# One core: k projected ahead of q, two sum banks from pair 4 on, small turns on sum banks, and GpSimd's multiplications on VectorE

## The chip, the core and the metric

The kernel runs on one core of one Trainium2 chip. The metric is device time in microseconds; the median of several runs is compared. The core has five engines with a queue each: TensorE (PE, with its weight loads as PEld), VectorE (DVE), ScalarE (ACT), GpSimd (POOL) and SyncE (SP, which here only starts transfers). Each queue runs in the order in which it was written; engines wait for one another by semaphores.

## What is computed

One layer of a trunk with two token mixers, on x of 1024 x 1024, all in float32:

```
h = rmsnorm(x, norm_g) * (1 + scale) + shift            # shift, scale, gate from c @ w_ada + b_ada
q_a, k_a, v_a, z_a, q_b, k_b, v_b, z_b, f_logit, g_logit = split(h @ w_in)
y_a = stick_breaking(q_a, k_a, v_a)                     # 8 heads of 64, strictly causal
y_a = (y_a * silu(z_a)) @ w_o_sb
cum_log_f = cumsum(log_sigmoid(f_logit + b_forget))
y_b = softmax(q_b k_b / 8 + cum_log_f[t] - cum_log_f[s]) v_b   # 8 heads of 64, causal
y_b = (y_b * silu(z_b)) @ w_o_fox
g = sigmoid(g_logit + b_gate)
merged = g[0] * y_a + g[1] * y_b
out = rmsnorm(x + gate * (merged @ w_out), final_g)
```

## The kernel before

Channels lie on the 128 partitions, and the 16 heads are worked through as 8 pairs: pairs 0 to 3 are the stick-breaking heads, 4 to 7 the forgetting ones. Every float32 product is made of three matmuls of split operands (a high part and a remainder). A projection unit fills one PSUM bank of 128x512 (an "acc" tile) with 24 matmuls, lines L181 to L183; the loads of its weights go through `load_w`.

For each pair p there are two runs of `attention(p, j)`, one for each head j. A run goes from the longest blocks of rows (m = 3) to the shortest (m = 0). A block computes its scores into z tiles (L623, L625; four banks in a ring, shared with the "tp" tiles for transposes), works them into weights on ACT and DVE (L690 to L726), sends the weights through a transposing transfer (wT) and, some steps later, multiplies them with v (`pv`, L756 and L757, into one bank "pv"). `turn` transposes the result (L776), gates it (L778) and stores it. Between the pieces of a run, a filler writes projection units into PE's queue: z, v, the merge gates and the next pair's q and k. So what stands between two blocks is the work of the next pair and of the gates. The steps at which `pv` and `turn` come are the numbers PVAT, PVFIRST, TURNAT and TURNEND; `sprinkle` puts small jobs (`load_v`, `largest`, `spread`, `take_v`) at counted steps of those units. The framework's scheduler then sets the final order on each engine, so that written order and run order can differ.

`largest` finds a power of two above the largest v of two pairs (transpose at L467, chain of small DVE operations up to vpow, L475); `spread` copies it to all partitions by a matmul (L480) and a copy (L482). `forget_gates` transposes the logits of the forget gate (L571). `residual_gate` sums a product of w_ada over eight loads (L599, gacc) and turns it with a matmul (L606). All four take a tp tile, one of the four of the z ring. `evac_q` and `evac_k` split a projected bank into two heads: on ACT the copies (L380, L383), on DVE the remainders (L381 for k, L384 for q); `evac_k` then starts the transfers kx<-ks (L404, L405) from GpSimd's queue. `evac_z` and `evac_g` do a chain on ACT and DVE (L409 to L413, then L423 for z); the last reader of a z bank is L423, that of a gate's bank of j < 8 is L412, and a gate of j >= 8 is only copied (L431).

The sum banks are a ring, and the v products have one bank that alternates only once "late" is set:

```
ring = {"next": 0, "of": 2, "pv": False, "late": False}
...
    ring["pv"] = ring["late"] and not ring["pv"]
    return acc_tile(2) if ring["pv"] else ps_pv.tile([P, 512], F32, name="pv", tag="pv")
...
    if b is None:
        b = ring["next"]
        ring["next"] = (b + 1) % ring["of"]
    return ps_acc.tile([P, 512], F32, name="acc", tag="acc%d" % b)
```

Until pair 7 the ring runs over three banks; then it has two, and the third takes every other v product. Pair 7's fill is the output projection of the first branch (`out_a`, L904 multiplies its sums with the gates in mA), then that of the second branch (`out_b`, L981 and L983), and at the end the product with w_out and the final norm.

Of the kernel before, what the change touches and what calls it, by code (L numbers as in the profile page):

```python
# [18 lines left out]
P = 128  # L19
S = 1024  # L20
D = 1024
HD = 64
# [27 lines left out]
T7 = (27, 27)  # L50
# [5 lines left out]
OUTQ = (0, 0)  # L56
LAGS = ((1, 2, 3, 4), (0, 1, 2, 3))
PVAT = (18, 16, 14, 10)
PVFIRST = 12
TURNAT = (22, 20, 18, 14)  # L60
TURNEND = (21, 19, 17, 13)

# [6 lines left out]
def tile_hybrid_block(ctx, tc, x, c, w_ada, b_ada, norm_g, w_in, b_forget,  # L69
# [380 lines left out]
        return (QA if p < 4 else QB) + (p % 4) * P  # L450

    def proj_qk(p):
        return proj(qcol(p), evac_q, p) + proj(qcol(p) + 512, evac_k, p)

    fT = [None]

# [6 lines left out]
    def largest(p):  # L463


        pt = tp_tile()
        nc.tensor.transpose(pt[0:1, :P], vmost[p], ident)  # L467
        top = at.tile([1, 1], F32, name="vtop", tag="vtop", bufs=2)
        nc.vector.tensor_reduce(top, pt[0:1, :P], mybir.AxisListType.X, ALU.max)
        nc.vector.tensor_scalar(top, top, 1e-25, None, ALU.max)  # L470
        e = top.bitcast(I32)
        nc.vector.tensor_scalar(e, e, 0x7F800000, None, ALU.bitwise_and)
        pair = vscale[p] = at.tile([1, 2], F32, name="vpow", tag="vpow", bufs=2)
        nc.vector.tensor_scalar(pair[:, 0:1].bitcast(I32), e, -1.0, float((254 + VSCALE) << 23), ALU.mult, ALU.add)
        nc.vector.tensor_scalar(pair[:, 1:2].bitcast(I32), e, 1.0, float((VSCALE + 15) << 23), ALU.mult, ALU.subtract)  # L475

    def spread(p):

        pt = tp_tile()
        nc.tensor.matmul(pt[:, 0:2], ones_row, vscale[p], start=True, stop=True)  # L480
        o = at.tile([P, 2], F32, name="vsc", tag="vsc", bufs=2)
        nc.vector.tensor_copy(o, pt[:, 0:2])  # L482
        for q in (p, p + 1):
            vscale[q], vback[q] = o[:, 0:1], o[:, 1:2]
# [82 lines left out]


    def forget_gates():
        pt = tp_tile()  # L570
        nc.tensor.transpose(pt[:64, :P], fT[0].rearrange("p h a -> p (h a)"), ident)  # L571
        fo = stage()[:64, 0:P]
        nc.vector.tensor_copy(fo, pt[:64, :P])
        nc.sync.dma_start(fd.rearrange("h (a t) -> (h a) t", a=TB), fo)
        fl = at.tile([8, S], F32, name="fl", tag="fb", bufs=2)
        nc.sync.dma_start(fl, fd)
        nc.vector.tensor_scalar(fl, fl, bfg, None, ALU.add)
        fa = at.tile([8, S], F32, name="fa", tag="fb", bufs=2)
        nc.scalar.activation(fa, fl, AF.Abs)
        nc.scalar.activation(fa, fa, AF.Exp, scale=-1.0)  # L580
        nc.scalar.activation(fa, fa, AF.Ln, bias=1.0)
        nc.vector.scalar_tensor_tensor(fa, fl, 0.0, fa, ALU.min, ALU.subtract)
        nc.vector.tensor_tensor_scan(fl, fa, fa, 0.0, ALU.add, ALU.bypass)
        nc.sync.dma_start(fd, fl)


    def residual_gate():

        box, raw = [], {}

        def load(k):
            raw[k] = load_raw(wada[k * P:(k + 1) * P, 2 * D:3 * D], [P, D])

        def weigh(k):
            if k == 0:
                box.append(at.tile([P, D], F32, name="gacc", tag="gacc"))
                nc.vector.tensor_scalar(box[0], raw[0], cT[:, 0:1], None, ALU.mult)
            else:
                nc.vector.scalar_tensor_tensor(box[0], raw[k], cT[:, k:k + 1], box[0], ALU.mult, ALU.add)  # L599

        def total(hf):
            t = slice(hf * 512, hf * 512 + 512)
            row = stage()[0:1, :]
            nc.sync.dma_start(row, b_ada[0:1, 2 * D + hf * 512:2 * D + hf * 512 + 512])
            ps = tp_tile()
            nc.tensor.matmul(ps[:1], ones, box[0][:, t], start=True, stop=True)  # L606
            nc.vector.tensor_add(row, ps[:1], row)
            nc.sync.dma_start(gated[:, t], row)
        return [lambda f=f, k=k: f(k) for k in range(KB) for f in (load, weigh)] + \
               [lambda hf=hf: total(hf) for hf in range(2)]  # L610
# [135 lines left out]
    def pv(pair):  # L746

        p, j, m = pair.p, pair.j, pair.m
        filler.finish(vunit.get(p))
        y = pv_tile()[:, 0:256].rearrange("p (a c) -> p a c", a=2)  # L750
        for a in (1, 0):
            nb = 2 * m + a + 1
            w, b = pair.wT[a], 2 * pair.at[a] // P
            for s in range(nb):
                v = vv[p][:, s, j, :]
                nc.tensor.matmul(y[:, a, :], w[:, b + s, :], v, start=s == 0, stop=False)  # L756
                nc.tensor.matmul(y[:, a, :], w[:, b + nb + s, :], v, start=False, stop=s == nb - 1)  # L757
        if j == 0 and m == 3:
            ysb[p] = at.tile([P, TB, P], F32, name="ysb", tag="ysb")
        o = ysb[p][:, 2 * m:2 * m + 2, j * HD:(j + 1) * HD]  # L760
        if p < 4:
            nc.scalar.activation(pair.fac, pair.low, AF.Exp, scale=-1.0)
        else:
            nc.vector.reciprocal(pair.fac, pair.fac)
        nc.vector.tensor_reduce(o, y.rearrange("p a (g d) -> p a d g", g=2), mybir.AxisListType.X, ALU.add)  # L765
        nc.gpsimd.tensor_mul(o, o, pair.fac.unsqueeze(2).to_broadcast((P, 2, HD)))  # L766

    def turn(p, m):

# [63 lines left out]
    yg, mA, merged = {}, [], []  # L833

    def gate_branch(p, hi, lo, raw=None):
        yg[p] = split(hi, lo, load_raw(yd[p], [P, S]) if raw is None else raw, p > 3 and p % 2 == 1)

    def load_ma(n):
        if n < 8:
# [110 lines left out]
    def out_b():  # L950
        pend = []

        def finish():
            m, hl, hf = pend.pop(0)
            split(hl[0][hf], hl[1][hf], m[:, hf * 512:hf * 512 + 512])

        gate = {}

        def load_gate(n):
            gate[n] = h_tile(F32, "gate")  # L960
            nc.sync.dma_start(gate[n], gd[8 + n])
            with tc.issue_after(last_exp[0].ins):
                nc.scalar.activation(gate[n], gate[n], AF.Sigmoid, bias=bg[:, 8 + n:9 + n])
        for n in range(GAHEAD):
            load_gate(n)
        for n in range(8):
            if n + GAHEAD < 8:
                load_gate(n + GAHEAD)
            if n % 2 == 0:
                w = wnext[0]  # L970
                if n < 6:
                    wnext[0] = wo_load(1, n + 2)
            g = gate[n]
            lo = h_tile(F32R, "mlo")
            hl = [two_halves("mrg"), [lo[:, 0:512], lo[:, 512:S]]]
            for hf in (1, 0) if n < 2 else (0, 1):
                t = slice(hf * 512, hf * 512 + 512)
                ps = part[n, hf] if n < 2 else z_tile()
                for _ in out_mm(ps, w, n, 1, t, (3,) if n < 2 else range(4)):
                    pass  # L980
                nc.vector.tensor_mul(g[:, t], ps, g[:, t])  # L981
                m = mA[n][:, t]
                (nc.vector if n > 5 else nc.gpsimd).tensor_add(m, m, g[:, t])  # L983
                pend.append((mA[n], hl, hf))
                if len(pend) > MLAG:
                    finish()
            merged.append(hl)
            for _ in range(WLOADS[n]):
                load_wout()
        while pend:  # L990
            finish()
# [32 lines left out]
    for p in range(7):  # L1024
        a, b = [], []
        if p == 0:
            g = sprinkle(gs.pop(0), [(6, lambda: load_v(0)), (8, lambda: largest(0)), (10, lambda: spread(0)),
                                     (13, lambda: take_v(0))])
            a += first_v + g
            vunit[0] = g[1]  # L1030
        else:
            a += proj_z(p)
            zunit[p] = a[-1]
# [5 lines left out]
            a.append(once(forget_gates))  # L1039
        b += proj_qk(p + 1)  # L1040
        q = p + 1
        marks = [(14, lambda q=q: largest(q)), (19, lambda q=q: spread(q))] if p % 2 else []
        sprinkle(b, [(12, lambda q=q: load_v(q))] + marks + [(24, lambda q=q: take_v(q))])
        if p == 6:
            a += b[:2]
            b[:2] = []
# [11 lines left out]
    for p in range(7):  # L1058
        for j in range(2):
            filler.last = plan[p, j][-1]  # L1060
            hooks = {2: lambda: forget_rows(p + j, 1 - j)} if (p, j) >= (3, 1) else {}
            attention(p, j, sum(u.steps for u in plan[p, j]), hooks)
            filler.finish(plan[p, j][-1])
            filler.last = None
    ring.update(next=0, of=2, late=True)
    start_a()
    filler.units += tail_a
    attention(7, 0, T7[0], {2: lambda: forget_rows(7, 1), 1: gate_b4})
    filler.units.append(once(gate_b, 5))
    attention(7, 1, T7[1])  # L1070
    gate_b(6)
    wnext[0] = wo_load(1, 0)
    filler.units += out_start()
    attention_end(TEND)
    filler.run(1000)
# [73 lines left out]
```

## Time and profile before

| | us |
|---|---|
| median of 3 runs (lowest to highest) | 947.38 (946.99 to 948.11) |
| profiled execution | 944.57 |
| its span | 942.9 |
| around the span | 1.67 |
| PE busy | 891.2 (95%) |
| DVE busy | 704.8 (75%) |
| ACT busy | 598.3 (63%) |
| POOL busy | 115.8 (12%) |

The profiled execution was 2.8 us shorter than the median; the span is the stretch from its first to its last instruction. Busy time counts overlapping instructions of one engine once. The numbers in brackets are shares of the span, and an engine that is busy little can still hold others up, since queues keep their order.

### The profile page before, as it was taken

The page shows a single profiled execution, that of the slowest core. Times are in us where ns is not written, and L with a number is a line of the kernel's source. Part 1 is how long each engine was busy: PE and PEld are TensorE (multiplying, and loading weights), DVE is VectorE, ACT ScalarE, POOL GpSimd, SP SyncE. Part 2 cuts the span into 40 slices and gives each one's busy share as a digit, 9 for nine tenths or more (in the row PEclk, how much of TensorE's full clock was granted, in tenths as well). Part 3 has the DMA queues.
Part 4 walks back from the last instruction along what each step waited for, and adds up shares of the span by engine and source line. Part 5 has one row for each costly group of instructions (what it writes and reads, how often), then busy time and mean ns, then how long its engine had stood idle before and what let it go on. Part 6 is the DMA issues. An engine that isn't in the chain of part 4 may idle for free. (4 is left out here: it accounts for less than half of the span.)

```text
span 942.9 us, 14905 instructions
## 1 busy us (share of the span) xinstructions
PE 891.2 (95%) x5282; PEld 753.0 (80%) x5282; DVE 704.8 (75%) x1402; ACT 598.3 (63%) x1102; POOL 115.8 (12%) x191
## 2 busy tenths in 40 slices
PE   2799999999999989999999999999999999999997
PEld 2688978889788868889878787897887777788886
DVE  4984998688786788878798768657687767776544
ACT  5656787776777697897678765445667456553222
POOL 0401001000010000100000112211212212540000
PEclk9999999999999989999999999999999999999999
DMA  9933495544594564936548697967999999552221
GB/s 313 305 98 101 100 225 122 127 104 121 132 193 121 143 152 112 176 82 133 147 121 187 175 211 157 210 160 188 192 203 173 279 263 213 201 178 90 101 92 54
DMA packets 260659, 152.14 MB, mean 161 GB/s; under 512 B 157156, under 2 KB 241748, under 8 KB 260584
## 3 DMA queue, kind: packets, MB, share of 16 engines
q1 hardware_dynamic: 257592, 142.78, 60.5%
q0 software_dynamic: 2880, 8.39, 4.9%
q8 instruction: 41, 0.67, 0.3%
q14 instruction: 34, 0.28, 0.1%
q10 hardware_dynamic: 112, 0.02, 0.0%
HBM read 80.31 MB, written 24.71 MB: 111 GB/s over the span
## 5 line engine op out<-in xcount | busy, mean ns | idle before, releaser
L181 PE MATMUL acc<-hhi,w 128*128 128x512 f32 x584 | 237.4, 406 | 0.0
L183 PE MATMUL acc<-hhi,w 128*128 128x512 f32 x584 | 230.0, 394 | 0.0
L182 PE MATMUL acc<-hlo,w 128*128 128x512 f32 x584 | 229.7, 393 | 0.0
L183 PEld LDWEIGHTS acc<-hhi,w 128*128 128x128 f32 x584 | 110.8, 190 | 24.6
L726 DVE SCALAR_TENSOR_TENSOR pc<-pw,pc 128x1024 f16<-128x1024 f32 (+7 forms) x128 | 96.6, 758 | 43.2 <-ACT pc L722 42.4
L181 PEld LDWEIGHTS acc<-hhi,w 128*128 128x128 f32 x584 | 111.4, 191 | 21.7 <-issue 2.0
L182 PEld LDWEIGHTS acc<-hlo,w 128*128 128x128 f32 x584 | 111.3, 191 | 19.6
L722 ACT ACTIVATE pc<-pw 128x1024 f16<-128x1024 f32 (+7 forms) x128 | 86.8, 679 | 19.2 <-DMA wT<-pc 17.8
L718 ACT ACTIVATE pw<-pw,low 128x1024 f32<-128x1024 f32 (+3 forms) x64 | 49.6, 776 | 73.3 <-DVE low L713 73.3
L766 POOL TENSOR_TENSOR ysb<-ysb,fac 128x128 f32<-128x128 f32 x64 | 35.6, 556 | 452.1 <-DVE ysb L765 388.1
L720 ACT ACTIVATE pw<-pw,low 128x1024 f32<-128x1024 f32 (+3 forms) x64 | 49.5, 774 | 62.1 <-DVE low L713 61.7
L530 PE MATMUL acc<-wv,hhi 128*128 128x256 f32 (+1 forms) x256 | 73.6, 288 | 0.0
L532 PE MATMUL acc<-wv,hlo 128*128 128x256 f32 (+1 forms) x256 | 72.4, 283 | 0.0
L531 PE MATMUL acc<-wv,hhi 128*128 128x256 f32 (+1 forms) x256 | 72.4, 283 | 0.0
L701 DVE SCALAR_TENSOR_TENSOR pw<-z,pw 128x512 f32<-128x512 f32 (+4 forms) x96 | 52.9, 553 | 23.1 <-ACT pw L692 22.6
L756 PE MATMUL pv<-vv,wT 128*128 128x128 f16 x534 | 66.6, 220 | 3.7 <-DVE ysb L765 3.7
L623 PE MATMUL z<-ks,qs 128*128 128x512 f32 (+1 forms) x192 | 66.4, 346 | 2.7 <-DVE yT L778 2.7
L625 PE MATMUL z<-kx,qs 128*128 128x512 f32 (+1 forms) x192 | 65.7, 344 | 3.4 <-DMA kx<-ks 3.4
L757 PE MATMUL pv<-vv,wT 128*128 128x128 f16 x534 | 66.5, 220 | 0.0
L166 DVE TENSOR_TENSOR w<-wraw,w 128x1024 fp32r<-128x1024 f32 x44 | 54.0, 1227 | 10.0 <-ACT w L165 8.8
L757 PEld LDWEIGHTS <-wT 128*128 128x128 f16 x576 | 56.6, 98 | 4.4 <-issue 4.1
L708 DVE TENSOR_TENSOR_SCAN pw<-pw 128x512 f32<-128x512 f32 (+2 forms) x64 | 58.9, 921 | 1.2
(276 smaller groups left out, 1985.8 us busy)
## 6 DMA issues: line engine op xcount, KB each, us to landing
wraw<-in_w_in_dram SPq DMA_DIRECT2D x48, 512.0 KB, 4.7
gd<-stg SPq DMA_DIRECT2D x32, 256.0 KB, 2.6
kx<-ks POOLq DMA_DIRECT2D x28, 256.0 KB, 6.4
ada<-in_w_ada_dram SPq DMA_DIRECT2D x12, 512.0 KB, 7.6
zd<-stg SPq DMA_DIRECT2D x16, 256.0 KB, 2.8
zt<-zd SPq DMA_DIRECT2D x32, 128.0 KB, 2.7
vraw<-vd SPq DMA_DIRECT2D x8, 512.0 KB, 3.9
fb<-fd SPq DMA_DIRECT2D x8, 512.0 KB, 4.6
```

What stands on the lines that cost most here:

```text
L181: nc.tensor.matmul(ps, w[0], x[0], start=first, stop=False)
L182: nc.tensor.matmul(ps, w[0], x[1], start=False, stop=False)
L183: nc.tensor.matmul(ps, w[1], x[0], start=False, stop=last)
L530: nc.tensor.matmul(ps[:, a], hhi[k][:, t], hi[:, k, :], start=k == 0, stop=False)
L531: nc.tensor.matmul(ps[:, a], hhi[k][:, t], lo[:, k, :], start=False, stop=False)
L532: nc.tensor.matmul(ps[:, a], hlo[k][:, t], hi[:, k, :], start=False, stop=k == KB - 1)
L623: nc.tensor.matmul(o, qs[p, j][:, tq], ks[p, j][:, s], start=True, stop=False)
L625: nc.tensor.matmul(o, qs[p, j][:, tq], kx[p, j][:, s], start=False, stop=not mask)
L722: nc.scalar.activation(pair.parts(a)[0], w, AF.Copy, scale=WSCALE)
L726: nc.vector.scalar_tensor_tensor(lo, pair.logits(a), WSCALE, hi, ALU.mult, ALU.subtract)
L756: nc.tensor.matmul(y[:, a, :], w[:, b + s, :], v, start=s == 0, stop=False)
L757: nc.tensor.matmul(y[:, a, :], w[:, b + nb + s, :], v, start=False, stop=s == nb - 1)
```

## The change

`proj_qk` writes the two k units ahead of the two q units. The ring is set to two banks, with "late", when pair 4 begins (it was pair 7), and the v products alternate between two banks from there. `largest`, `spread`, `forget_gates` and `residual_gate` take the next sum bank, not a slot of the z ring. The marks of `spread` and `take_v` move by some steps, and PVFIRST by one. 64 multiplications with fac (L766), one remainder of `gate_branch` and 12 additions to mA (L983) go from GpSimd to DVE. `gate_b(5)`, `gate_b(6)` and the first weights of `out_b` are taken up inside the runs of pair 7.

```diff
-PVFIRST = 12
+PVFIRST = 13
...
     def proj_qk(p):
-        return proj(qcol(p), evac_q, p) + proj(qcol(p) + 512, evac_k, p)
+        return proj(qcol(p) + 512, evac_k, p) + proj(qcol(p), evac_q, p)
...
     def largest(p):
-        pt = tp_tile()
+        pt = acc_tile()
...
     def spread(p):
-        pt = tp_tile()
+        pt = acc_tile()
...
     def forget_gates():
-        pt = tp_tile()
+        pt = acc_tile()
...
-            ps = tp_tile()
+            ps = acc_tile()
             nc.tensor.matmul(ps[:1], ones, box[0][:, t], start=True, stop=True)
...
-        nc.gpsimd.tensor_mul(o, o, pair.fac.unsqueeze(2).to_broadcast((P, 2, HD)))
+        nc.vector.tensor_mul(o, o, pair.fac.unsqueeze(2).to_broadcast((P, 2, HD)))
...
     def gate_branch(p, hi, lo, raw=None):
-        yg[p] = split(hi, lo, load_raw(yd[p], [P, S]) if raw is None else raw, p > 3 and p % 2 == 1)
+        yg[p] = split(hi, lo, load_raw(yd[p], [P, S]) if raw is None else raw)
...
-                (nc.vector if n > 5 else nc.gpsimd).tensor_add(m, m, g[:, t])
+                nc.vector.tensor_add(m, m, g[:, t])
...
-            g = sprinkle(gs.pop(0), [(6, lambda: load_v(0)), (8, lambda: largest(0)), (10, lambda: spread(0)),
-                                     (13, lambda: take_v(0))])
+            g = sprinkle(gs.pop(0), [(6, lambda: load_v(0)), (7, lambda: largest(0)), (12, lambda: spread(0)),
+                                     (15, lambda: take_v(0))])
...
-        marks = [(14, lambda q=q: largest(q)), (19, lambda q=q: spread(q))] if p % 2 else []
-        sprinkle(b, [(12, lambda q=q: load_v(q))] + marks + [(24, lambda q=q: take_v(q))])
+        marks = [(14, lambda q=q: largest(q)), (23, lambda q=q: spread(q))] if p % 2 else []
+        sprinkle(b, [(12, lambda q=q: load_v(q))] + marks + [(28, lambda q=q: take_v(q))])
...
+            if (p, j) == (4, 0):
+                ring.update(next=0, of=2, late=True)
             attention(p, j, sum(u.steps for u in plan[p, j]), hooks)
...
-    ring.update(next=0, of=2, late=True)
     start_a()
     filler.units += tail_a
-    attention(7, 0, T7[0], {2: lambda: forget_rows(7, 1), 1: gate_b4})
-    filler.units.append(once(gate_b, 5))
-    attention(7, 1, T7[1])
-    gate_b(6)
-    wnext[0] = wo_load(1, 0)
+    attention(7, 0, T7[0], {2: lambda: forget_rows(7, 1), 1: gate_b4, 0: lambda: gate_b(5)})
+
+    def load_b():
+        wnext[0] = wo_load(1, 0)
+    attention(7, 1, T7[1], {2: lambda: gate_b(6), 1: load_b})
```

Three places on PE's queue. The first is in pair 2, at the transpose of the forget gates; one piece of the difference, - before and + changed.

```order
 L182 MATMUL acc<-hlo,w 128x512
 L183 MATMUL acc<-hhi,w 128x512
-L571 MATMUL tp<-ident,fT 64x128
+L571 MATMUL acc<-ident,fT 64x128
 L623 MATMUL z<-ks,qs 128x256
 L625 MATMUL z<-kx,qs 128x256
```

The order stays, and the transpose's tile is now one of the three sum banks, no longer one of the four of the z ring.

The second is the end of pair 3, in the change and in the kernel before. acc_5338 is the last half of a gate's projection (j < 8); acc_5447 and acc_5489 are the two halves of z of pair 4, written in this order; the z tiles belong to scores. Before:

```order
L181 MATMUL acc_5338<-hhi_156,w_5154 128x512
L182 MATMUL acc_5338<-hlo_164,w_5154 128x512
L183 MATMUL acc_5338<-hhi_156,w_5154 128x512
L623 MATMUL z_5427<-ks_3835,qs_3695 128x256
L625 MATMUL z_5427<-kx_3836,qs_3695 128x256
L627 LDWEIGHTS ident16_136
L627 MATMUL z_5427<-mask16_138,ident16_136 128x128
L181 MATMUL acc_5447<-hhi_149,w_5273 128x512
L182 MATMUL acc_5447<-hlo_157,w_5273 128x512
L183 MATMUL acc_5447<-hhi_149,w_5273 128x512
```

Changed:

```order
L181 MATMUL acc_5489<-hhi_150,w_5273 128x512
L182 MATMUL acc_5489<-hlo_158,w_5273 128x512
L183 MATMUL acc_5489<-hhi_150,w_5273 128x512
L181 MATMUL acc_5489<-hhi_151,w_5273 128x512
L182 MATMUL acc_5489<-hlo_159,w_5273 128x512
L183 MATMUL acc_5489<-hhi_151,w_5273 128x512
L623 MATMUL z_5507<-ks_4918,qs_5072 128x512
L625 MATMUL z_5507<-kx_4919,qs_5072 128x512
L181 MATMUL acc_5447<-hhi_149,w_5273 128x512
L182 MATMUL acc_5447<-hlo_157,w_5273 128x512
L183 MATMUL acc_5447<-hhi_149,w_5273 128x512
```

Before, unit 5447 follows 5338 after one short score. Changed, with 5447 on the bank that 5338 had, nine matmuls of 5489 and the scores z_5476 and z_5507 go ahead of it.

The third is the end of pair 5, at `spread` (L480). acc_6936 before is the first k unit of pair 6; changed, acc_6942 (the first q unit, further up) and acc_7044 (the second) are the q units, and acc_7183 is the first half of z of pair 6. Before:

```order
L181 MATMUL acc_6936<-hhi_150,w_6788 128x512
L182 MATMUL acc_6936<-hlo_158,w_6788 128x512
L183 MATMUL acc_6936<-hhi_150,w_6788 128x512
L606 MATMUL tp_6970<-gacc_5877,ones_117 1x512
L181 MATMUL acc_6936<-hhi_151,w_6788 128x512
L182 MATMUL acc_6936<-hlo_159,w_6788 128x512
L183 MATMUL acc_6936<-hhi_151,w_6788 128x512
L480 MATMUL tp_6978<-vpow_6905,rows_121 128x2
L181 MATMUL acc_6936<-hhi_152,w_6788 128x512
L182 MATMUL acc_6936<-hlo_160,w_6788 128x512
L183 MATMUL acc_6936<-hhi_152,w_6788 128x512
```

Changed:

```order
L623 MATMUL z_7167<-ks_5891,qs_6079 128x256
L625 MATMUL z_7167<-kx_5892,qs_6079 128x256
L181 MATMUL acc_7183<-hhi_149,w_6939 128x512
L182 MATMUL acc_7183<-hlo_157,w_6939 128x512
L183 MATMUL acc_7183<-hhi_149,w_6939 128x512
L181 MATMUL acc_7183<-hhi_150,w_6939 128x512
L480 MATMUL acc_7009<-vpow_6907,rows_121 128x2
L182 MATMUL acc_7183<-hlo_158,w_6939 128x512
L183 MATMUL acc_7183<-hhi_150,w_6939 128x512
L181 MATMUL acc_7183<-hhi_151,w_6939 128x512
L181 MATMUL acc_7044<-hhi_149,w_6788 128x512
L182 MATMUL acc_7044<-hlo_157,w_6788 128x512
```

Before, the two small turns stand in the middle of a unit, on tp tiles. Changed, the matmul of `spread` stands behind the unit acc_6942 on its bank, four matmuls of the next unit are drawn ahead of it, and acc_7044 follows on the same bank.

At the end of pair 6 the first q unit of pair 7 moves in the same way behind two scores of the second head and seven matmuls of a v product.

## Rows read from the trace of the kernel before

**Rows 1.** The page, part 1: busy time, share, instructions.

```profile
PE 891.2 (95%) x5282; PEld 753.0 (80%) x5282; DVE 704.8 (75%) x1402; ACT 598.3 (63%) x1102; POOL 115.8 (12%) x191
```

**Rows 2.** Waits of PE: line, releaser, us in total, times, longest us.

```profile
PE tp L480 <- DVE vpow L475: 4.1, 3, 2.2
PE pv L756 <- DVE ysb L765: 3.7, 2, 2.0
PE z L625 <- DMA kx<-ks: 3.4, 1, 3.4
PE acc L181 <- DVE mA L904: 3.3, 4, 1.4
PE acc L181 <- ACT yah L165: 3.1, 2, 1.6
PE z L623 <- DVE yT L778: 2.7, 1, 2.7
...
PE acc L182 <- POOL ybl L166: 1.2, 1, 1.2
```

**Rows 3.** Seven stretches: length, busy (x) PE, PEld, DVE, ACT, POOL; clock.

```profile
346.70:353.50 6.80, 6.32 (x16) 5.04 (x17) 4.45 (x14) 5.45 (x14) 0.65 (x1) 0.50 0.59 149
470.00:485.00 15.00, 12.80 (x83) 10.39 (x82) 14.09 (x27) 12.20 (x18) 0.40 (x1) 1.00 0.45 112
515.00:520.00 5.00, 5.00 (x23) 4.13 (x22) 4.73 (x11) 4.88 (x13) 0.71 (x1) 1.00 0.24 95
534.40:537.80 3.40, 3.40 (x19) 2.92 (x17) 3.16 (x9) 2.62 (x6) 1.79 (x3) 0.50 0.95 172
592.40:595.90 3.50, 3.50 (x11) 2.68 (x10) 0.21 (x1) 0.00 (x0) 0.00 (x0) 0.51 1.18 262
662.35:664.00 1.65, 1.65 (x32) 1.65 (x31) 1.58 (x3) 1.48 (x3) 0.00 (x0) 1.00 0.00 0
816.00:925.00 109.00, 109.00 (x477) 89.40 (x477) 66.79 (x122) 36.13 (x65) 16.79 (x10) 1.00 0.31 107
```

**Rows 4.** Timeline of PE, one that waited, and first matmuls of four units.

```profile
356.58 0.48 PE L181 MATMUL acc<-hhi,w 128*128 128x512 f32 x1
...
477.03 0.27 PE L480 MATMUL tp<-vpow,rows 1*128 1x2 f32 x1 [2.20 <-DVE vpow L475]
...
514.71 0.48 PE L181 MATMUL acc<-hhi,w 128*128 128x512 f32 x1
...
644.90 0.39 PE L181 MATMUL acc<-hhi,w 128*128 128x512 f32 x1
...
695.66 0.40 PE L181 MATMUL acc<-hhi,w 128*128 128x512 f32 x1
```

**Rows 5.** Timeline of DVE: the last reader of a sum bank, and others.

```profile
352.35 0.75 DVE L412 SCALAR_TENSOR_TENSOR stg<-acc,nbg,stg 128x512 f32<-128x512 f32 x1 [2.35 <-ACT stg L411]
...
479.18 0.69 DVE L384 SCALAR_TENSOR_TENSOR qs<-acc,qs 64x512 fp32r<-64x512 f32 x1
...
520.65 0.76 DVE L412 SCALAR_TENSOR_TENSOR stg<-acc,nbg,stg 128x512 f32<-128x512 f32 x1 [0.88 <-ACT stg L411]
521.32 0.28 DVE L701 SCALAR_TENSOR_TENSOR pw<-z,pw 128x128 f32<-128x128 f32 x1
...
595.69 1.28 DVE L599 SCALAR_TENSOR_TENSOR gacc<-wraw,cols,gacc 128x1024 f32<-128x1024 f32 x1 [4.90 <-DMA wraw<-in_w_ada_dram]
...
600.81 0.68 DVE L423 TENSOR_TENSOR stg<-acc,stg 128x512 f32<-128x512 f32 x1
...
649.44 0.69 DVE L384 SCALAR_TENSOR_TENSOR qs<-acc,qs 64x512 fp32r<-64x512 f32 x1
...
699.02 1.30 DVE L384 SCALAR_TENSOR_TENSOR qs<-acc,qs 64x512 fp32r<-64x512 f32 x2
```

**Rows 6.** Groups of instructions by shape: line, form, xcount; busy, mean ns; idle before.

```profile
L983 POOL TENSOR_TENSOR mA<-mA,gate 128x512 f32<-128x512 f32 x12 | 19.4, 1635 | 13.6 <-DVE gate L981 8.6 <-DMA wraw<-in_x_dram 2.9 <-ACT woh L165 2.1
...
L983 DVE TENSOR_TENSOR mA<-mA,gate 128x512 f32<-128x512 f32 x4 | 2.8, 691 | 0.1
```

## Prediction

> **What bounds the kernel now.** The page's first part comes first: PE is busy 891.2 of 942.9 us, DVE 75%, POOL 12% [rows 1]. So the kernel is bound by PE's queue, and an edit is worth what it takes from PE's idle time, or what it adds to it. Next come PE's waits. Leaving out the first 50 us, which the change does not touch, they are few and each has its place: three times `spread` (4.1 us), two products with v (3.7), one score that waits for its transfer kx (3.4), one behind the forget gates (2.7), and some 8 us in pair 7 [rows 2]. Last, the stretches: after three of these waits the granted clock stood at half for 6.8, 3.4 and 3.5 us, from 346.7, 534.4 and 592.4; after the 2.20 us wait at 477 it stayed full [rows 3, 4]. Half clock is 1.2 GHz in place of 2.4, so each such stretch costs half its length: 3.4, 1.7 and 1.7 us. The reader should see that removing a wait of 2 to 3 us can return the clock's price too, and that a new wait of that size can take it.
>
> **What a sum bank costs.** A projection's matmul takes about 0.22 us in PE's queue (23 in 5.00 us), so a unit of 24 takes about 5.4 us, and a product with v about 0.05 us (32 in 1.65) [rows 3]. A bank is free when its last reader is done, which is late: the gate unit before 514.71 has its last reader from 520.65 to 521.41, 6.7 us later, and the q unit that ends at about 644.9 has its from 649.44 to 650.13, 5.2 us later [rows 4, 5]. With three banks two further units lie between the end of a unit and the next use of its bank, some 11 us. With two banks one unit does, 5.4 us, about the same as the time until the last reader. And where a small turn takes a bank, the ring goes on by one, so that the next unit can meet the bank that was filled just before it. This is the price of the change, and the order of the changed kernel shows the scheduler moving units back for it.
>
> **The terms, in order of time** (minus is a gain).
>
> Pair 0, `spread`: it stands some steps later, so its vpow is ready. Of about 1.0 us of waiting (4.1 less the two others, of which the longest is 2.2 [rows 2]) all or none can go, since it now needs a sum bank too; I take half, -0.5. Pair 1: the same, 0, with -0.8 and +0.8 as bounds.
>
> Pair 2, forget gates: the transpose leaves the z ring, so the score behind it no longer waits for yT. That removes 2.7 us and the half clock behind it, 3.4: -6.1 [rows 2, 3]. But the transpose and two units behind it now go round the three banks, and the last of them needs the bank whose reader L412 runs from 352.35 to 353.10 [rows 5]. PE began that unit at 356.58 [rows 4]; 6.1 less is 350.5, so 2.6 us come back: -3.5. Bounds: -6.1 if the reader runs earlier too, -1.5 if the wait is long enough to halve the clock.
>
> Pair 3, `spread`: it waited 2.20 us for vpow [rows 4]. Now it waits for a q bank whose last reader, L384, ends at 479.87 [rows 5], and it stands some 4 matmuls further on, at about 477.85 less what was gained: +0.1, between -2.2 and +1.8.
>
> End of pair 3: the first unit after 514.71 is moved behind nine matmuls and four scores, about 2.9 us, so PE comes to it at 517.6, and its bank is free at 521.41: a wait of 3.8 us. It is longer than those that halved the clock, so 1.7 may come on top. Against it, the wait of a v product (2.0) and its half clock (1.7) go, since the products alternate over two banks from here [rows 2, 3]. Between +0.1 and +1.8 I take +1.0; lower bound -2, if the reader's chain comes earlier.
>
> Pair 4: the other v product's wait (1.7), the wait for kx (3.4) and its half clock (1.7) go: -6.8 [rows 2, 3]. k first means that kx is started two units earlier, about 11 us, against 3.4 that are missing. But here DVE itself waits: L599 stands 4.90 us for its part of w_ada and starts at 595.69, and behind it in DVE's queue the z bank's last reader ends at 601.49 [rows 5]. With two banks, the unit after next needs this bank; if L599 moves by nothing, PE loses all 6.8 again, and if the load comes earlier (kx no longer shares the transfer engines with it) it loses little. Halfway: -3.2; bounds -6.8 and +1.
>
> Pair 5 into 6, the third place of the order: the units q0, `spread`, q1 stand on one bank. Ahead of q0 there are 9 scores, 20 products and two L606, about 5 us against 5.2 until the reader is done: +0.3. Ahead of `spread` 7 scores, 30 products and four matmuls, 4.0 us: +1.2. Behind q1 only 17 matmuls, 3.8 us, until the first score of pair 6, which now needs q last, not kx: +1.4. Together +2.9, between 0 and +6 (clock halved twice) [rows 3, 5]. Before, there was no wait of PE here.
>
> Pair 6: q0 of pair 7 stands behind 4 scores and 7 products more than the unit that began at 695.66 [rows 4], so at about 697.0; the bank's remainders ended at 700.32 [rows 5]. The wait is between 0 and 3.3; I take +1.7.
>
> Pair 7: the remainder ybl on POOL held PE for 1.2 us; taken up earlier and on DVE, it goes: -1.2. The 12 multiplications L766 in this pair come ahead of L904 on DVE, for which PE waited 3.3 us [rows 2]: four waits by less than 0.1 us more, since most lie behind a wait that is longer, +0.2. Together -1.0, bounds -2.5 and +1.
>
> GpSimd's work on DVE: a 128x128 operation on DVE took 0.28 us [rows 5], so 64 of L766 are 18 us of DVE, and 12 of L983 at 0.69 are 8.3 us [rows 6]. DVE has 238 us idle in the span [rows 1], and in 816 to 925, where L983 stands, it was busy 66.8 of 109.0 us while PE was busy all 109.0 [rows 3]. So both are hidden by PE's own work; if that cover were gone, all 26 us would count. GpSimd needed 1.635 us for an addition that took DVE 0.691 [rows 6]. The Trainium skill, page "SBUF — State Buffer", section "Who interferes with whom", says that a DVE instruction with two inputs in SBUF contends with GpSimd instructions that read SBUF; that agrees with the slow GpSimd rows, and by it DVE would get some time back. As PE is the bound there, the sum would be the same up to a gain of the +0.2 above.
>
> **Sum.** -0.5 - 3.5 + 0.1 + 1.0 - 3.2 + 2.9 + 1.7 - 1.0 = -2.5 us. The profiled execution of 944.57 (942.9 and 1.67 around it) becomes 942.1; it lies 2.8 us under the median, and on the median's scale 947.38 becomes 944.9.
>
> **Rivals.** *Two banks suffice.* If the readers come as early as PE needs them, the waits go and nothing returns: -0.5 - 6.1 - 3.7 - 6.8 - 1.2 = -18.3, so 929.1; half of that, 938, is as near. For it: DVE and ACT have idle time in pairs 4 to 6, and the scheduler has drawn other work ahead. Against it: the readers' ends are chains over ACT and DVE, 5 to 7 us long. *The bank chain decides (slower).* At the end of pair 5 each of the steps q0, `spread`, q1 waits for the whole 5.2 us, less what is ahead, and the readers come later since L766 is among DVE's work: +6 in place of +2.9, and at the end of pair 4 nothing is gained (0, not -3.2): +3.8, so 951.2. It decides from the point at which the three waits together pass some 6 us. For it: the order; against it: DVE had room there. *The clock.* New waits of 2 us and more, up to four of them (pair 3's end, pair 5 twice, pair 6), each with 3.4 us at half clock: +6.8 less the +0.8 counted, 950.9. For it: three of the four waits of about 2 us or more between the start and pair 7 halved it [rows 2, 3]; against it: the one at 477 did not. The Trainium skill, page "TensorE: Matmul & The Clock Gate", section "A second HAM failure mode: psum-queue depth-cycling", tells of a kernel whose cycling through banks left short idles that let the clock swing; no row here shows that from waits below 2 us. *Nothing moves:* the waits change places, 947.4 within 1.9.
>
> **Chances.** Forecast 0.40 (its own range 942 to 947.4), two banks suffice 0.20, bank chain 0.17, clock 0.09, nothing moves 0.14. A measurement of this kernel can tell 0.2%, 1.9 us. Of the forecast's 0.40 about 0.27 lies more than 1.9 us below; with the first rival that is 0.48 faster (0.01 from elsewhere); 0.27 same (0.13 and the 0.14); 0.25 slower. The range goes from 932, inside the first rival, to 952, beyond the two slower ones.
>
> **What would show it.** Right: no wait for kx at the end of pair 4 and none behind the forget gates; no v product that waits for L765; waits of the first matmul of a unit at the ends of pairs 3, 5 and 6, of 1 to 4 us, for DVE's last reader of the bank; PE's waits after 50 us shorter by 2 to 4 us in all. Wrong: if these unit waits are missing (then it is the first rival) or if they pass 10 us in all, or if L599 still ends late and the z bank with it.

## The result, and the profile after

The changed kernel is slower: 960.22 us (median of 6 runs, 954.47 to 963.20) against 946.29 for the kernel before (6 runs, 942.24 to 948.11); ratio 1.0148, interval 1.0124 to 1.0173. The forecast was 944.9, 2.5 us below the kernel before, in a range from 932 to 952. The profiled execution took 963.20 us, span 961.5, the longest of the six, so its span is 18.6 us above that of before where the medians differ by 13.9. What follows from the two traces is therefore up to 4.7 us more than what the medians show.

The page of the changed kernel, its span and its first part:

```profile
span 961.5 us, 14787 instructions
...
PE 898.8 (93%) x5282; PEld 756.4 (79%) x5282; DVE 722.2 (75%) x1479; ACT 598.9 (62%) x1102; POOL 62.7 (7%) x114
```

PE is idle 62.7 us in place of 51.7 [rows 1], and busy 7.6 us longer with the same 5282 instructions: together the 18.6. Its waits, with the start left out (line, releaser, total us, times, longest):

```profile
PE acc L181 <- DVE stg L412: 6.2, 3, 4.4
...
PE z L623 <- DVE mx L713: 4.4, 3, 1.8
PE acc L530 <- DVE stg L423: 4.2, 1, 4.2
PE acc L480 <- DVE ks L381: 3.6, 2, 2.3
PE acc L480 <- DVE qs L384: 2.7, 1, 2.7
PE tp L776 <- DVE ysb L766: 2.6, 2, 2.3
...
PE acc L181 <- DVE mA L895: 1.5, 1, 1.5
...
PE acc L181 <- DVE mA L904: 0.8, 2, 0.6
PE pv L756 <- DVE ysb L765: 0.7, 1, 0.7
```

Against [rows 2], the waits for kx, ybl and yah are gone, those of v products fell from 3.7 to 0.7 us, those for mA at L904 from 3.3 to 0.8, with a new one of 1.5 at L895. In their place PE waits for last readers of sum banks: L412, L423, L381, L384. After the first 50 us all waits of PE add up to 32.8 us, where before they were 22.7. The granted clock after these waits, in six stretches of the changed kernel (columns as in [rows 3]):

```profile
423.00:426.40 3.40, 3.40 (x10) 2.63 (x9) 3.40 (x7) 2.04 (x3) 0.00 (x0) 0.50 0.23 77
525.40:528.80 3.40, 3.40 (x9) 2.63 (x8) 2.48 (x7) 3.13 (x6) 0.00 (x0) 0.50 0.28 93
614.20:621.00 6.80, 5.56 (x25) 5.56 (x26) 2.96 (x6) 1.77 (x3) 0.21 (x1) 0.50 0.58 144
675.60:679.00 3.40, 3.40 (x10) 2.62 (x9) 3.01 (x10) 1.76 (x7) 0.40 (x1) 0.50 0.57 164
716.60:720.00 3.40, 3.40 (x9) 2.66 (x8) 3.20 (x13) 1.37 (x4) 1.61 (x3) 0.51 1.09 296
829.20:832.60 3.40, 3.40 (x10) 2.63 (x9) 2.60 (x5) 1.02 (x2) 0.00 (x0) 0.50 0.74 276
```

They add up to 23.8 us at half clock against 13.7 in [rows 3]. PE was busy for 22.6 us of them, before for 13.2; half of the difference, 4.7 us of the 7.6 of longer busy time, is the clock's. (The stretch from 614.20 begins while PE still waits, so its price is half of 5.56 us, 2.8, and not 3.4.) PE at five of the longer waits:

```profile
354.75 0.50 PE L181 MATMUL acc<-hhi,w 128*128 128x512 f32 x1 [1.55 <-DVE stg L412]
...
421.91 0.44 PE L623 MATMUL z<-ks,qs 128*128 128x448 f32 x1 [1.81 <-DVE mx L713]
...
525.08 0.53 PE L181 MATMUL acc<-hhi,w 128*128 128x512 f32 x1 [4.42 <-DVE stg L412]
...
615.44 0.58 PE L530 MATMUL acc<-wv,hhi 128*128 128x256 f32 x1 [4.18 <-DVE stg L423]
...
674.03 0.24 PE L480 MATMUL acc<-vpow,rows 1*128 1x2 f32 x1 [2.70 <-DVE qs L384]
```

DVE ahead of the wait at 615, in the changed kernel:

```profile
609.75 1.28 DVE L599 SCALAR_TENSOR_TENSOR gacc<-wraw,cols,gacc 128x1024 f32<-128x1024 f32 x1 [2.21 <-DMA wraw<-in_w_ada_dram]
610.96 0.28 DVE L766 TENSOR_TENSOR ysb<-ysb,fac 128x128 f32<-128x128 f32 x1
611.16 1.22 DVE L166 TENSOR_TENSOR w<-wraw,w 128x1024 fp32r<-128x1024 f32 x1
...
612.89 0.69 DVE L412 SCALAR_TENSOR_TENSOR stg<-acc,stg 128x512 f32<-128x512 f32 x1
...
614.70 0.69 DVE L423 TENSOR_TENSOR stg<-acc,stg 128x512 f32<-128x512 f32 x1 [0.35 <-ACT stg L413]
```

L599 waits for a part of w_ada; the bank's readers L412 and L423 stand behind it, and PE behind them. In the kernel before, the same L599 (the last one) did not wait, and the same L423 (the twelfth in both kernels) held nobody up:

```profile
601.48 1.26 DVE L599 SCALAR_TENSOR_TENSOR gacc<-wraw,cols,gacc 128x1024 f32<-128x1024 f32 x1
...
608.61 0.69 DVE L423 TENSOR_TENSOR stg<-acc,stg 128x512 f32<-128x512 f32 x1 [0.35 <-ACT stg L413]
```

Where the span went: the start of the n-th score matmul (L623, counted through the program; both kernels have 192) in the two traces.

| score | before | changed | difference |
|---|---|---|---|
| 43rd (pair 1) | 270.02 | 272.24 | +2.2 |
| 61st (pair 2) | 356.09 | 352.51 | -3.6 |
| 79th (pair 3) | 436.34 | 438.18 | +1.8 |
| 103rd (pair 4) | 540.39 | 545.72 | +5.3 |
| 133rd (pair 5) | 636.27 | 645.67 | +9.4 |
| 145th (pair 6) | 669.77 | 686.03 | +16.3 |
| 169th (pair 7) | 727.67 | 748.33 | +20.7 |
| 192nd (pair 7) | 792.53 | 809.35 | +16.8 |

### The profile page after: what moved, and what is told of

Read it like the earlier page. It is cut to its first block, busy times and chain, and to the rows that moved or that the text cites. A ratio compares the mean times of both kernels' runs of the same rounds, so it can differ in the third digit from the quotient of the medians.

```text
span 961.5 us, 14787 instructions
## 1 busy us (share of the span) xinstructions
PE 898.8 (93%) x5282; PEld 756.4 (79%) x5282; DVE 722.2 (75%) x1479; ACT 598.9 (62%) x1102; POOL 62.7 (7%) x114
## 4 chain that ended last, share of the span: by engine, by line
PE 41%; DVE 11%; DMA 8%; ACT 6%; issue 4%; SPq 1%; DVEq 0%; ACTq 0%
PE acc L181 6%; PE acc L183 6%; PE acc L182 6%; PE z L183 4%; PE z L182 4%; PE z L181 4%; DMA wT<-pc 2%; DVE pw L708 2%; DMA wraw<-in_w_ada_dram 2%; DVE pw L701 1%; PE z L623 1%; PE z L625 1%; DVE pw L713 1%; PE acc L530 1%; PE acc L531 1%
## 5 line engine op out<-in xcount | busy, mean ns | idle before, releaser
L718 ACT ACTIVATE pw<-pw,low 128x1024 f32<-128x1024 f32 (+3 forms) x64 | 49.7, 776 | 82.1 <-DVE low L713 81.9
L720 ACT ACTIVATE pw<-pw,low 128x768 f32<-128x768 f32 (+4 forms) x64 | 49.4, 772 | 60.7 <-DVE low L713 60.5
L530 PE MATMUL acc<-wv,hhi 128*128 128x256 f32 (+1 forms) x256 | 74.9, 292 | 4.2 <-DVE stg L423 4.2
L531 PE MATMUL acc<-wv,hhi 128*128 128x256 f32 (+1 forms) x256 | 73.5, 287 | 0.0
L623 PE MATMUL z<-ks,qs 128*128 128x512 f32 (+1 forms) x192 | 66.8, 348 | 5.7 <-DVE mx L713 4.4
L756 PEld LDWEIGHTS <-wT 128*128 128x128 f16 x576 | 55.7, 98 | 3.8 <-issue 3.0
L757 PEld LDWEIGHTS <-wT 128*128 128x128 f16 x576 | 56.4, 98 | 1.5 <-issue 1.3
L165 ACT CAST w<-wraw 128x1024 fp32r<-128x1024 f32 (+2 forms) x46 | 47.1, 1023 | 14.5 <-DMA wraw<-in_w_in_dram 6.4
L756 PE MATMUL pv<-vv,wT 128*128 128x128 f16 x450 | 55.3, 219 | 0.7 <-DVE ysb L765 0.7
```

The lines of the kernel that those rows point to most:

```text
L530: nc.tensor.matmul(ps[:, a], hhi[k][:, t], hi[:, k, :], start=k == 0, stop=False)
L531: nc.tensor.matmul(ps[:, a], hhi[k][:, t], lo[:, k, :], start=False, stop=False)
L623: nc.tensor.matmul(o, qs[p, j][:, tq], ks[p, j][:, s], start=True, stop=False)
```

## The experiments

Ratios are to the kernel before, timed on the same chip; its medians lay between 944.9 and 946.9 us. The diffs are to the changed kernel unless it is said otherwise. First, one part undone at a time.

**Three banks again until pair 7.**

```diff
-            if (p, j) == (4, 0):
-                ring.update(next=0, of=2, late=True)
...
+    ring.update(next=0, of=2, late=True)
     start_a()
```

> The changed kernel with one part undone: the ring keeps three banks until pair 7 and the v products have their one bank until then, as before. Theory 1 (two banks are the cause: PE comes to a bank before its last reader L412, L423, L384 or L381 is done, and each wait of 2 us or more then halves the clock): the waits of the changed trace at 525, 615, 674 and 716 go, 4.4 + 4.2 + 2.7 + 1.2 us and some 8.5 us of half clock, and 2 to 4 us come back at the v products: 942 to 948. Theory 2 (the small turns on sum banks are the cause, whatever the number of banks): 955 to 960. Theory 3 (k ahead of q) and theory 4 (DVE's added work makes the readers late): 956 to 960.

944.18 us, ratio 0.9987 (0.9971 to 1.0003). Theory 1: the whole loss hangs on the switch ahead of pair 7, to two sum banks and a second bank for v products. (Its clause on the clock does not hold as put: in the changed trace a wait of 2.33 us at 482 left the clock at full.) The rest of the change, gains and losses, then comes to nothing that can be told.

**The small turns back in the z ring.** In `largest`, `spread`, `forget_gates` and `residual_gate` (where the tile is called `ps`):

```diff
-        pt = acc_tile()
+        pt = tp_tile()
```

> The changed kernel with one part undone: the four small turns take a slot of the z ring again, not a sum bank. Theory 2: the waits of L480 (6.3 us with 1.7 to 3.4 us of half clock) and L606 (1.4) go and the sum ring is no longer shifted under the q and k units: 948 to 951. Theory 1: the waits for two banks stay in other places, and the score behind the forget gates waits for yT again (2.7 and 3.4 of clock): 956 to 962. Theories 3 and 4: 957 to 962.

952.57 us, 1.0080 (1.0052 to 1.0109), somewhat above theory 2's 948 to 951. L480 waits 0.1 us, and the gain at the forget gates is gone, as is the wait at 421. About half of the loss needs the small turns on sum banks.

**q ahead of k again.**

```diff
-        return proj(qcol(p) + 512, evac_k, p) + proj(qcol(p), evac_q, p)
+        return proj(qcol(p), evac_q, p) + proj(qcol(p) + 512, evac_k, p)
```

> The changed kernel with one part undone: q is projected ahead of k again. Theory 3 (with k first, k finds no free ks or kx tile and q is the last thing that the next pair's scores need, so banks are held longer): 952 to 956. Theory 1, 2 and 4: within 3 us of the changed kernel, or slower, as the scores wait for kx again: 958 to 966.

954.40 us, 1.0099 (1.0074 to 1.0123): in theory 3's range. A third of the loss needs k first.

**L766, L983 and the remainder of `gate_branch` on GpSimd again.**

```diff
-        nc.vector.tensor_mul(o, o, pair.fac.unsqueeze(2).to_broadcast((P, 2, HD)))
+        nc.gpsimd.tensor_mul(o, o, pair.fac.unsqueeze(2).to_broadcast((P, 2, HD)))
...
-                nc.vector.tensor_add(m, m, g[:, t])
+                (nc.vector if n > 5 else nc.gpsimd).tensor_add(m, m, g[:, t])
```

> The changed kernel with one part undone: L766, L983 and the remainder of gate_branch (odd p above 3) run on GpSimd again. Theory 4 (18 us of DVE work put ahead of the readers of the sum banks): 951 to 956. Theories 1 to 3: within 2 us of the changed kernel, or slower by the 1.2 us of ybl: 958 to 963.

959.44 us, 1.0156 (1.0132 to 1.0181). Theory 4 falls: DVE's added work costs nothing that shows in the time, though it moves single waits (below).

Then the parts alone and together.

**On the kernel before, two banks from pair 4 alone.**

```diff
+            if (p, j) == (4, 0):
+                ring.update(next=0, of=2, late=True)
             attention(p, j, sum(u.steps for u in plan[p, j]), hooks)
...
-    ring.update(next=0, of=2, late=True)
     start_a()
```

> The kernel before with one part of the change alone: the ring goes to two banks, and the v products to two, from pair 4 on. Theory 1 (two banks cost by themselves, whatever is projected first and wherever the small turns go): 952 to 958 against 945. Theory 5 (they cost only together with the small turns on sum banks and with k first, which shift the units onto the bank that was filled just before): 943 to 948.

947.82 us, 1.0038 (1.0021 to 1.0055). Within theory 5's 943 to 948: two banks alone cost 0.4%, and the other 1.1% need company.

**On the kernel before, k first alone** (the third diff reversed).

> The kernel before with one part of the change alone: k projected ahead of q. If the wait for kx at the end of pair 4 (3.4 us and 1.7 of half clock) is what it removes and nothing replaces it: 939 to 942. If the scores then wait for q, or the k units for their tiles, as long: 944 to 948.

946.71 us, 1.0012 (0.9994 to 1.0030): no change to be told. The wait for kx is gone from its trace, and others have come, 1.84 us of a score for L713 at 587 among them. So the gain that the prediction saw in this wait is not there even with three banks.

**Both undone: small turns in the z ring and q first, two banks kept.**

> The changed kernel with two parts undone: the small turns in the z ring and q ahead of k; two banks from pair 4 on stay. If the parts add up (7.6 and 5.8 us came back when each was undone alone): 945 to 948. If the two hang on one another so that undoing both gives no more than undoing one: 951 to 955. The kernel before with two banks alone ran at 947.8.

948.99 us, 1.0027 (1.0011 to 1.0043). The parts add up: 0.68% and 0.49% undone singly, 1.21% together. What is left is about what two banks cost alone.

**Three banks, and only the forget gates on a sum bank** (first diff, and the second without `forget_gates`).

> The changed kernel with three sum banks until pair 7, and with only the transpose of the forget gates left on a sum bank; the other small turns take a slot of the z ring again. Theory 1 with theory 2 (the ring and the turns of spread cost, the rest gains): the waits of L480 (4.3 us and 3.4 of half clock with three banks) and L606 (1.4) go, and the gain at the forget gates stays: 932 to 938. If waits only change places: 941 to 946.

943.97 us, 0.9982 (0.9961 to 1.0003): a miss for the 932 to 938. The waits changed places: at 422 a score waits 1.78 us, at 527 L776 waits 2.07 us, at 570 a v product 1.97 us.

**The same with L766 on GpSimd.**

> As the run with three banks and only the forget gates on a sum bank, and L766 on GpSimd again. If the new waits of the transposes L776 for L766 in pair 7 (2.5 us, 1.7 of half clock in one execution) come from L766 standing in DVE's queue: 1 to 4 us below that run. If DVE's added work costs nothing or GpSimd is as late: within 1 us of it.

945.10 us, 0.9992 (0.9976 to 1.0008): no gain. L776 in pair 7 then waits 2.8 us for L766 on GpSimd, so the engine is not the reason of that wait.

**Small turns on the next sum bank, without moving the ring.**

```diff
-        pt = acc_tile()
+        pt = acc_tile(ring["next"])
```

> The changed kernel, but a small turn takes the sum bank that comes next without moving the ring on, so that the units alternate over the two banks as if there were no small turns. Theory P (the small turns cost because they shift the ring, and a unit meets the bank that was filled just before it): 951 to 955, like the run with all small turns in the z ring (952.6). Theory O (they cost because they occupy and wait for a sum bank at all): 957 to 962.

958.29 us, 1.0138 (1.0116 to 1.0159): theory O. The unit behind the turn now waits for the turn's reader, 2.58 us at 259, 2.47 at 475 and at 655, each followed by half clock. (The profile puts the first two down to L711, which ran right behind the reader: L482 at 258.64, L469 at 474.83.) So a small turn on a sum bank costs by what it waits for or what waits for it, whether it shifts the ring or not. 

**The loads of w_ada one mark earlier.**

```diff
-        return [lambda f=f, k=k: f(k) for k in range(KB) for f in (load, weigh)] + \
+        work = [(load, 0)] + [x for k in range(KB - 1) for x in ((load, k + 1), (weigh, k))] + [(weigh, KB - 1)]
+        return [lambda f=f, k=k: f(k) for f, k in work] + \
```

> The changed kernel, but each of the eight loads of w_ada for the residual gate is started one mark ahead of the product before it, not right ahead of its own. Theory L (in the changed trace DVE stands 2.2 us at L599 for such a load and, behind it, L412 and L423 come late, so that PE waits 4.2 us at 615 for the z bank and 3.4 us follow at half the clock price): 952 to 955. If the readers of that bank are late without it, or the wait only moves: 957 to 962.

955.64 us, 1.0113 (1.0081 to 1.0145): 0.35% back, just outside the range of theory L (952 to 955), and the interval overlaps that of the changed kernel, so by the time alone it cannot be told from nothing. The wait at 615 did shrink, from 4.18 us to this (PE and DVE of that kernel; the lines behind L609 are one higher there):

```profile
601.11 1.29 DVE L599 SCALAR_TENSOR_TENSOR gacc<-wraw,cols,gacc 128x1024 f32<-128x1024 f32 x1 [0.92 <-DMA wraw<-in_w_ada_dram]
602.32 0.68 DVE L412 SCALAR_TENSOR_TENSOR stg<-acc,stg 128x512 f32<-128x512 f32 x1
...
603.70 0.69 DVE L423 TENSOR_TENSOR stg<-acc,stg 128x512 f32<-128x512 f32 x1
...
604.45 0.39 PE L530 MATMUL acc<-wv,hhi 128*128 128x256 f32 x1 [0.75 <-DVE stg L423]
```

and no half clock follows it. What comes back is less than the 7.0 us of that place (4.18 of wait, 2.8 of clock): a v product now waits 2.42 us for its transposed weights, and the chain at the end of pair 5 stays (2.69 us for `spread`). In this execution `spread` of pair 3, which the edit does not touch, waits 3.28 us with 6.8 us of half clock, 2.33 us and none in the changed kernel's: single executions differ by that much.

**v products on one bank until pair 7, two sum banks kept.**

```diff
-                ring.update(next=0, of=2, late=True)
+                ring.update(next=0, of=2)
...
+    ring.update(late=True)
     start_a()
```

> The changed kernel, but the v products stay on one bank until pair 7, so that from pair 4 on the third sum bank is not used by anything. If the second bank for v products is worth what the waits for L765 cost before (3.7 us and 1.7 of half clock): 963 to 967. If PE waits for the sum banks anyway and the v products are hidden in that: 958 to 962.

961.16 us, 1.0177 (1.0152 to 1.0201): 0.3% above the changed kernel, with overlapping intervals. What the second bank for v products wins is too little to be told.

Now open: where in pairs 4 to 6 the loss arises.

**The switch at pair 5, and at pair 6** (in the condition of the first diff, (5, 0) and (6, 0)).

> The changed kernel, but the switch to two sum banks and two banks for v products comes at pair 5, not pair 4. If each pair pays its own price (the waits that begin at the end of pair 3 and in pair 4 are 4.4 + 1.7 and 4.2 + 3.4 us with the clock, less some 4 us that the v products win): 948 to 952. If the price is paid once, where pairs 5 to 7 meet, wherever the switch stands: 957 to 961.

> The changed kernel, but the switch comes at pair 6. If each pair pays its own price: 944 to 949, below the run with the switch at pair 5, since the chain of spread between the q units at the end of pair 5 (6.7 us with the clock) goes too. If the price is paid once: as the run with the switch at pair 5.

961.61 us, 1.0154 (1.0120 to 1.0188), and 948.63 us, 1.0013 (0.9993 to 1.0033). Two banks in pair 4 as well cost nothing that can be told: with the switch at pair 5 the 4.42 us at 525 are gone, but a v product waits 1.64 us at 569 again, and the wait at 614 is longer. Pair 5 makes the difference, 1.4%. With the switch at pair 5 PE's waits there are 5.49 us for L423 at 614 (6.8 us of half clock around it), 2.54 for L713 at 667, 2.69 for `spread` at 673; with the switch at pair 6 none of the three is there.

**Small turns in the z ring and the early loads.**

> The changed kernel with the small turns back in the z ring and with the loads of w_ada one mark earlier. If what k first costs with two banks is the bank held behind L599's load (4.2 us at L423, with the clock): 944 to 948, as with q first (949.0). If it lies elsewhere: 950 to 954, near the run with only the small turns undone (952.6).

942.79 us, 0.9962 (0.9945 to 0.9979). With k first and two banks, and faster than the kernel before: the early loads are worth 1.2% here, where the small turns don't stand in the way. The wait at L530 is 0.78 us in place of 4.23. This does not show yet that all of it is the bank held behind L599: the early loads also gain 0.7% on the kernel before (below), which has no such wait. About 0.5% is left, as much as k first cost (1.0148 to 1.0099), which fits but is not shown by itself.

**Three banks, forget gates on a sum bank, early loads, and L766 of pair 7 on GpSimd.**

> The run with three banks and only the forget gates on a sum bank (944.0), with the loads of w_ada one mark earlier and L766 of pair 7 on GpSimd. If these two remove waits of PE (2.4 us of L776 with 1.7 us of half clock, and some of the waits for z tiles in pair 4): 938 to 942, below both kernels. If the waits only move: 943 to 946.

939.33 us, 0.9915 (0.9889 to 0.9942): beats both kernels.

**On the kernel before, the early loads alone.**

> The kernel before with one thing of its own: the loads of w_ada one mark earlier. If with three banks the late load is covered (no bank is needed while DVE stands at L599): 944 to 948, and the gain of the run with three banks and early loads (939.3 against 946.1) comes from the changed parts. If the early loads alone make it: 938 to 942.

939.78 us, 0.9929 (0.9904 to 0.9953), against my first reading, that with three banks the late load is covered. The earlier loads alone make nearly all of the best version's gain. Waits of PE in this trace, against [rows 2]:

```profile
PE tp L480 <- DVE vpow L475: 4.3, 3, 2.3
PE acc L181 <- DVE mA L905: 4.0, 4, 2.0
PE z L624 <- DVE yT L779: 2.7, 1, 2.7
...
PE pv L757 <- DVE ysb L766: 1.7, 2, 1.5
```

The wait for kx (3.4 us) is gone, with one of the v products' (1.99 us at 534), and so are the two stretches of half clock behind them. DVE shows one place. In the kernel before, ahead of the reader L765 for which the v product at 534 waited:

```profile
527.50 1.28 DVE L599 SCALAR_TENSOR_TENSOR gacc<-wraw,cols,gacc 128x1024 f32<-128x1024 f32 x1 [1.25 <-DMA wraw<-in_w_ada_dram]
...
533.70 0.42 DVE L765 TENSOR_REDUCE ysb<-pv 128x128 f32<-128x256 f32 x1
```

With the early loads this L599 had started at 517.03, without a wait, and the reader (one line lower in that kernel) comes 3.2 us sooner:

```profile
530.50 0.42 DVE L766 TENSOR_REDUCE ysb<-pv 128x128 f32<-128x256 f32 x1
```

The last reader of k ahead of kx then runs at 581.30 in place of 587.64. How much of these 6 us came from the first place, and how much from the waits of L599 between, was not separated.

**The best version with two banks from pair 4.**

> The run with three banks, early loads and L766 of pair 7 on GpSimd (939.3), but with two sum banks and two banks for v products from pair 4 on. If two banks cost only through the load and the small turns: 935 to 941, as the v products no longer wait. If they cost by themselves, 0.3 to 0.4 per cent: 942 to 945.

946.25 us, 1.0009 (0.9990 to 1.0028): 0.9% above the same kernel with three banks. Here two banks cost without the late loads and with only the forget gates' turn on a sum bank (k first is still there), and more than alone on the kernel before. At 517 a score waits 3.17 us and at 525 a unit 2.22 us for L412, with 6.8 and 3.4 us of half clock; with three banks neither wait is there, but v products wait 2.56 and 2.19 us for the last reader of their bank.

## Why the prediction was wrong

**Right in kind.** The bound, PE's queue; that the waits for kx, ybl and the score behind the forget gates would go; that new waits would stand at the ends of pairs 3, 5 and 6, for the last reader of a bank (4.42 us; 2.70, though at `spread` and not at a unit; 1.16); that GpSimd's work is hidden on DVE (L766 took 286 ns there, for the 280 assumed; undoing it moved nothing).

Of the signs of being wrong that it named, two came: the waits for banks at those places and in pair 5 (4.42, 4.18, 2.70, 1.16) pass 10 us in all, and an L599 ended late, with a z bank behind it.

**Term by term.** Pairs 0 and 1: -0.5 forecast, +2.2 at the 43rd score, of which 0.8 stood already at the first. Forget gates: -3.5 forecast; from the 43rd to the 61st score the trace gains 5.8 us, of which 1.55 (at 354.75) come back: -4.2. But at the end of pair 2 a score waits 1.81 us for a z tile, with 3.4 us of half clock behind it: +3.5, which no term had. The wait is there, though the half clock is not always, with three banks, with q first, with early loads and in the best version, all of which have this transpose on a sum bank; with the small turns in the z ring it is not, and with L766 on GpSimd it is 0.29 us. So it needs the transpose on a sum bank and L766 on DVE, and even these two do not make it alone: with the small turns on a sum bank that does not move the ring it is not there. Pair 3, `spread`: +0.1 forecast, 2.33 us of wait in place of 2.20. End of pair 3: +1.0 forecast, taken between +0.1 and +1.8; the wait came out at 4.42 us, for 3.8, and the half clock with it, less the v product's 2.0 and 1.7: +2.4. Pair 6: +1.7 forecast, +4.4 from the 145th to the 169th score, of which waits of 0.55, 0.45 and 1.16 us and 1.7 of clock are 3.9. Pair 7: -1.0; from the 169th score to the end -2.1.

**The step that failed first** is the term of pair 4: "if L599 moves by nothing, PE loses all 6.8 again, and if the load comes earlier ... it loses little. Halfway: -3.2". The bounds were -6.8 and +1; from the 103rd to the 133rd score the trace lost 4.1 us, 7.3 more than the term has. The loads did not come earlier but later: the last two were issued at 595.00 and 603.20, where before it was 587.63 and 597.00. The L599 that I had read (4.90 us before) did not wait, and its bank's reader, L423 at 602.11, held nobody up. The wait came one place later, behind the last L599: 4.18 us and 2.8 of clock, which is as much as the gain of 6.8; and new waits for z tiles and for banks of q and k, 3.1 us from 577 to 596, come on top. So even the bad bound of +1 was too good, since it took only what could be lost of the gain. I saw the mechanism and priced it at half of its range, which has no ground: nothing in the change starts that load sooner. What this chain costs in the time of the whole kernel is not shown by itself: early loads take back 1.2% with the small turns undone (1.0080 to 0.9962), of which they gain 0.7% on the kernel before too.

**The second** is pair 5 into 6: +2.9 forecast, +6.9 measured (0.47 and 0.88 for L606, 0.94 for a score, 2.70 for `spread`, 1.7 of clock). I counted for each unit the PE work ahead of it at full length, and left out of the middle value that the readers move later with the waits and that the clock can fall: it did so behind the 2.70 us. The run with the switch at pair 6 has none of this, nor the wait of L530, and costs 0.13%, no change that can be told; it does not part the two.

**The third** is that the terms were summed as if each stood alone. Two rivals, the bank chain and the clock, were each priced near 951, as alternatives; they came together. All but the switch is worth -0.1%, the switch alone +0.4%, both +1.5%. And gains counted as waits that go were not gains: k first alone takes the wait for kx away and moves the time by 0.1%, less than can be told.

**What stays open.** Why two banks cost 0.9% in the best version and 0.4% alone on the kernel before; the orders differ in many places. How the parts that make the z tile late at 421 act together: no L766 runs on DVE between 409.3 and this wait, and no run moved that tile alone. How the loss of 1.5% divides over the chain behind L599 and the end of pair 5.

## What to carry to other kernels

A ring with fewer banks is only as good as the latest reader, so before taking one away look at each reader's place in its own queue: one operation at the head of VectorE's queue that waits for a load (here 2.21 us) holds every bank whose reader stands behind it. Starting those loads earlier, an edit of one place, gained 0.7% on the kernel before, although none of TensorE's waits there named them. A term whose price hangs on whether a transfer comes earlier should be taken at its bad end unless the edit starts that transfer sooner.

## What the runs showed of the hardware

Of PE's waits in the traces shown, one of 2.20 us left the clock at 2.4 GHz and one of 1.99 us was followed by 3.4 us at 1.2 GHz [rows 3, 4]; in the changed kernel 1.81 us at 421.91 and 1.16 us at 716 (with 0.55 and 0.45 in the 3.5 us ahead of it) were too, while 2.33 us at 482 was not. In this kernel the length of the one wait does not tell. The Trainium skill, page "TensorE: Matmul & The Clock Gate", section "A second HAM failure mode: psum-queue depth-cycling", tells of short idles between matmul groups that make the clock swing; the changed trace agrees, with six stretches of half clock in place of three (the first 50 us and the last 3 of each trace left out).

With GpSimd's additions on DVE, DVE's own remainders mlo beside them became shorter: 868 ns on average before, 686 after, and 867 with the additions back on GpSimd. The Trainium skill, page "SBUF — State Buffer", section "Who interferes with whom", has that a DVE instruction with two inputs in SBUF contends with GpSimd's reads; these numbers agree. It moved no time here (1.0156 with them back, 1.0148 without), as PE was the bound.
